# A hybrid decoder layer on one core: two groups of 128x128 transposes taken off TensorE and done by moving 32-row pieces and turning 32x32 blocks

## The chip, the cores and the metric

The kernel runs on one core of a Trainium2 chip. Such a core has five engines that take their own instruction streams in order and meet through semaphores: TensorE (PE in the profile; its weight loads are PEld), VectorE (DVE), ScalarE (ACT), GpSimd (POOL) and SyncE (SP), which here only issues DMAs. The metric is the device time of one execution in microseconds. The median of three runs of the kernel before is 1166.14 us (1165.94 to 1166.46).

## The reference

One decoder layer on x of 2048 tokens by 1024 channels, float32. A normalised x goes through one input projection of 4096 columns. 3072 of them are q, k, v and a gate of 12 attention heads of 64; 1024 feed a short gated convolution. The attention is a mixture of three dilated windows, each over a band of keys; the group outputs are concatenated, projected back to 1024, normalised and added to x.

```python
h = rmsnorm(x, norm_pre_g)
z = jnp.einsum('bsd,de->bse', h, w_in)
q, k, v, g_attn, c_h, c_b, c_c, g_conv = jnp.split(z, cuts, axis=-1)
q = rope(q.reshape(B, S, N_ATTN_HEADS, HEAD_DIM), pos)
k = rope(k.reshape(B, S, N_ATTN_HEADS, HEAD_DIM), pos)
for window, dilation in ((128, 1), (512, 4), (2048, 16)):
    o_i, lse_i = dilated_window_attn(q, k, v, window, dilation)   # scores, exp, sum, p @ v
o = sum over the three of softmax(lse)_i * o_i
attn_out = o * silu(g_attn)
conv_out = c_b * causal_depthwise_conv(c_c * c_h, conv_w) * silu(g_conv)
y = jnp.einsum('bse,ed->bsd', concatenate([attn_out, conv_out]), w_out)
return x + rmsnorm(y, norm_post_g)
```

## The kernel before, in words

The 2048 tokens are cut into four chunks of 512 (`b` = 0 to 3). The 4096 input columns are cut into eight groups of 512 (`grp`): groups 0 and 7 are the convolution, groups 1 to 6 are pairs of heads (k, q, v and gate, 128 columns each). A unit is one group for one chunk: there are 32, of which 24 are attention units, and six of those are of the first chunk. Groups are the outer loop and chunks the inner one, so every fourth attention unit is a first-chunk unit.

Every product is done in two parts, a rounded high part and the rest (`fp32r` tiles with two halves), as three matmuls: high by high, high by low, low by high (L1072 to L1074 for the projection). So whatever is fed to TensorE is first split: ScalarE copies with rounding, VectorE subtracts.

In an attention unit the projections of k, q, v and the gate land in four PSUM banks (`zs`), with channels on the partitions and tokens along the row. k and q are rotated, q on VectorE and GpSimd (L707, L711). v has to stand the other way round, tokens on the partitions: ScalarE (L696; for the first chunk VectorE, L698) brings it to SBUF as `vz`, TensorE turns it by four 128x128 transposes into a PSUM bank (`vt`, L739), and L744 and L745 split it from there. Scores are matmuls with 64 rows (L772 for the dilated windows, L800 for the near one). VectorE takes each row's minimum with the mask (L779, L807), ScalarE the exponential (L783, L811). The probabilities then have queries on the partitions and must be turned before they meet v: `parts` does it for the dilated windows. Its `far` branch, used for chunks 2 and 3 only, turns 32x32 blocks in place on VectorE (L831), which suffices there by the layout; its other branch and `square`, for the near window, use four TensorE transposes into a PSUM bank (L840, L863), from which ScalarE and VectorE split (L845, L846; L870, L873, L877). Then come the products with v (L889; L900 to L902 for the near window), whose results are gathered in SBUF (L920 to L925).

Nothing of the order is left to the hardware. `add` records each step with its engine, an estimated duration, a priority and what it reads and writes; `Plan.schedule` walks through estimated time and gives each engine the ready step of the lowest priority number, and `emit` writes the steps out in that order. A table `SHIFT` nudges the priority of steps by line and unit. So a change of one step's estimate or of the table reorders instructions on all engines. TensorE fills its time between the parts of one unit's attention with the projection of the next unit.

## Time and profile before

| | |
|---|---|
| median of three runs | 1166.14 us |
| the profiled execution: its own time, its span | 1165.18 us, 1163.1 us |
| TensorE, VectorE, ScalarE, GpSimd busy | 1152.5, 960.3, 668.2, 199.7 us |
| transposes of v (L739) | 96 |
| transposes of probabilities outside `far` (L840, L863) | 336 and 192 |
| granted TensorE clock | 0.998 |

The span runs from the first to the last instruction of the program; the device time lies 2.1 us above it. A busy TensorE is counted by overlapping, modelled ends of pipelined matmuls, so its busy share does not tell how tightly the matmuls follow each other; the chain of waits does, where each matmul stands with the time that passes until the next. A VectorE or ScalarE row's mean is the length of one instruction, and back to back they overlap a little, so the group's busy time divided by its count is what one costs in a full queue.

### The profile page before, as it was taken

The page shows a single profiled execution, that of the slowest core. Times are in us where ns is not written, and L with a number is a line of the kernel's source. Part 1 is how long each engine was busy: PE and PEld are TensorE (multiplying, and loading weights), DVE is VectorE, ACT ScalarE, POOL GpSimd, SP SyncE. Part 2 cuts the span into 40 slices and gives each one's busy share as a digit, 9 for nine tenths or more (in the row PEclk, how much of TensorE's full clock was granted, in tenths as well). Part 3 has the DMA queues.
Part 4 walks back from the last instruction along what each step waited for, and adds up shares of the span by engine and source line. Part 5 has one row for each costly group of instructions (what it writes and reads, how often), then busy time and mean ns, then how long its engine had stood idle before and what let it go on. Part 6 is the DMA issues. An engine that isn't in the chain of part 4 may idle for free.

```text
span 1163.1 us, 19964 instructions
## 1 busy us (share of the span) xinstructions
PE 1152.5 (99%) x6422; PEld 958.3 (82%) x6422; DVE 960.3 (83%) x2424; ACT 668.2 (57%) x1722; POOL 199.7 (17%) x158
## 2 busy tenths in 40 slices
PE   9999999999999999999999999999999999999997
PEld 7888888888888888888888888888888888888885
DVE  4744588997999989898999998997999888688876
ACT  6743365665666556666665565674667454544442
POOL 0001112212131222121223221203222103000000
PEclk9999999999999999999999999999999999999999
DMA  9977786787688767777777767688776968445452
GB/s 345 391 278 261 247 247 212 226 236 230 203 247 269 234 215 227 238 223 242 232 245 229 252 167 247 204 272 260 228 243 199 318 208 297 156 149 178 152 165 91
DMA packets 174136, 269.39 MB, mean 232 GB/s; under 512 B 53584, under 2 KB 109904, under 8 KB 174032
## 3 DMA queue, kind: packets, MB, share of 16 engines
q1 hardware_dynamic: 173472, 267.85, 71.1%
q8 instruction: 51, 0.84, 0.3%
q14 instruction: 53, 0.43, 0.1%
q10 hardware_dynamic: 560, 0.27, 0.1%
HBM read 206.77 MB, written 48.69 MB: 220 GB/s over the span
## 4 chain that ended last, share of the span: by engine, by line
PE 94%; DVE 2%; ACT 2%; DMA 1%; SPq 0%; issue 0%; POOL 0%; DVEq 0%; POOLq 0%; ACTq 0%
PE st L1072 20%; PE st L1074 19%; PE st L1073 19%; PE st L889 5%; PE st L1241 4%; PE st L1243 4%; PE st L1242 4%; PE st L772 4%; PE st L800 3%; PE st L840 3%; PE st L901 2%; PE st L863 2%; PE st L548 1%; PE st L902 1%; PE st L739 1%; PE st L900 1%
## 5 line engine op out<-in xcount | busy, mean ns | idle before, releaser
L1072 PE MATMUL st<-xt,w 128*128 128x512 f32 x1020 | 413.3, 405 | 0.0
L1074 PE MATMUL st<-xt,w 128*128 128x512 f32 x1020 | 399.7, 392 | 0.0
L1073 PE MATMUL st<-xt,w 128*128 128x512 f32 x1020 | 398.3, 391 | 0.0
L1074 PEld LDWEIGHTS st<-xt,w 128*128 128x128 f32 x1020 | 191.5, 188 | 42.4
L1072 PEld LDWEIGHTS st<-xt,w 128*128 128x128 f32 x1020 | 191.9, 188 | 40.4 <-issue 6.7
L1073 PEld LDWEIGHTS st<-xt,w 128*128 128x128 f32 x1020 | 192.1, 188 | 31.1
L783 ACT ACTIVATE p<-p,sm 128x128 f32<-128x128 f32 (+3 forms) x192 | 105.9, 553 | 69.2 <-DVE sm L779 69.0
L925 DVE TENSOR_TENSOR uu<-st,uu 64x256 f32<-64x256 f32 x288 | 115.0, 418 | 26.0 <-ACT uu L920 21.8
L920 ACT COPY uu<-st 64x256 f32<-64x256 f32 x192 | 67.2, 367 | 100.7 <-PE st L889 55.9
L1019 POOL TENSOR_TENSOR uu<-uu 128x512 f32<-128x512 f32 x24 | 37.4, 1557 | 359.0 <-DVE uu L1018 359.0
L811 ACT ACTIVATE p<-p,e 128x256 f32<-128x256 f32 (+1 forms) x192 | 94.4, 495 | 5.0 <-DVE e L807 4.8
L779 DVE CUSTOM_DVE_ANT_0 p<-st,cst 128x128 f32<-128x128 f32 (+3 forms) x192 | 82.1, 485 | 16.1 <-PE st L772 15.7
L889 PEld LDWEIGHTS st<-pt,v 128*128 128x128 f32 x480 | 66.7, 191 | 5.6
L807 DVE CUSTOM_DVE_ANT_0 p<-st,cst 128x256 f32<-128x256 f32 (+1 forms) x192 | 66.8, 412 | 4.2 <-PE st L800 4.2
L889 PE MATMUL st<-pt,v 128*128 128x256 f32 x480 | 68.5, 283 | 0.0
L870 ACT ACTIVATE pt<-st 128x512 fp32r<-128x512 f32 (+1 forms) x96 | 51.1, 585 | 24.2 <-PE st L863 20.7
L707 DVE TENSOR_TENSOR rp<-rp,cs 128x512 f32<-128x512 f32 x72 | 53.7, 772 | 12.9 <-DMA rp<-rp 12.7
L707 POOL TENSOR_TENSOR rp<-rp,cs 128x512 f32<-128x512 f32 x24 | 39.5, 1646 | 143.1 <-DMA rp<-rp 96.9
L846 DVE TENSOR_TENSOR pt<-st,pt 128x512 fp32r<-128x512 f32 x84 | 55.9, 683 | 5.0 <-ACT pt L845 4.7
L772 PE MATMUL st<-kk,q 64*128 64x128 f32 (+3 forms) x576 | 56.3, 333 | 0.3 <-DVE v L745 0.2
L772 PEld LDWEIGHTS st<-kk,q 64*128 64x128 f32 x576 | 42.4, 185 | 15.1 <-issue 10.8
L845 ACT CAST pt<-st 128x512 fp32r<-128x512 f32 x84 | 46.8, 581 | 9.0 <-PE st L840 8.4
(262 smaller groups left out, 2045.6 us busy)
## 6 DMA issues: line engine op xcount, KB each, us to landing
xt<-xt SPq DMA_DIRECT2D x256, 512.0 KB
raw<-in_w_in SPq DMA_DIRECT2D x59, 256.0 KB
rp<-rp SPq DMA_DIRECT2D x192, 64.0 KB
vd<-v SPq DMA_DIRECT2D x24, 512.0 KB
v<-vd SPq DMA_DIRECT2D x96, 128.0 KB
ab<-ad SPq DMA_DIRECT2D x48, 256.0 KB
cs<-in_rope SPq DMA_DIRECT2D x19, 512.0 KB
uu<-mix SPq DMA_DIRECT2D x26, 256.0 KB
```

The costliest lines, as they stand in the source:

```text
L707: add(e, dur, pr, lambda o=o, a=a, i=i, eng=eng: eng.tensor_tensor(o.ap, a.ap, cs.ap[:, i], op=ALU.mult), r=[cs], w=[o], port=True)
L772: mm(ps[h].ap[:, (r - r0) * w:(r - r0 + 1) * w], Q.ap[lo:lo + 64, i, r * 128:(r + 1) * 128], KK[j][lo:lo + 64, 4 * r:4 * r + 4, 0:w // 4]. ...
L779: add("DVE", dvet(w) + 0.01, pr + URG, lambda h=h, r=r, P4=P4: vec.tensor_tensor_reduce(P4.ap[:, r, 0:w], ps[h].ap[:, (r - r0) * w:(r - r0 ...
L783: add("ACT", actt(w) + 0.19, pr, lambda h=h, r=r, P4=P4: act.activation(P4.ap[:, r, 0:w], P4.ap[:, r, 0:w], AF.Exp, bias=s4(0, h)[:, r:r + ...
L807: add("DVE", dvet(256) + 0.01, pr + URG, lambda h=h, j=j, g=g, P1=P1: vec.tensor_tensor_reduce(P1.ap[:, g, lo[g]:], ps[h].ap[:, j * 256 + ...
L811: add("ACT", actt(256 - lo[g]) + 0.19, pr, lambda h=h, g=g, P1=P1: act.activation(P1.ap[:, g, lo[g]:], P1.ap[:, g, lo[g]:], AF.Exp, bias=E ...
L889: mm(dst, v, pt.ap[:, i], start=c == 0, stop=c == b, skip_group_check=False)
L920: add("ACT", actt(256, True) + 0.09, pr + URG, lambda: act.copy(cols(a, lo), o()[hi:hi + 64, 0]), r=[O], w=[(a, (h, half))])
L925: fn = lambda l=l: vec.tensor_tensor(cols(a, lo), o()[lo:lo + 64, l], cols(a, lo), op=ALU.add)
L1072: mm(z.ap, w.ap[:, 0, js], xt.ap[:, 0], start=kt == 0, stop=False)
L1073: mm(z.ap, w.ap[:, 0, js], xt.ap[:, 1], start=False, stop=False)
L1074: mm(z.ap, w.ap[:, 1, js], xt.ap[:, 0], start=False, stop=kt == KT - 1)
```

## The change

Two transposes are replaced.

**v.** `vt` and its PSUM bank go. Sixteen ScalarE instructions per unit each take 32 partitions of v (for chunks 1 to 3 straight from the projection's PSUM bank, with the factor 0.5 that L696 applied; for the first chunk from `vz`) and write 128 values a row to another block of 32 partitions of `vq`, so that the 32x32 blocks stand at their transposed places. One VectorE transpose then turns all blocks in place. The split reads `vq` in SBUF.

**The first chunk's probabilities.** For `b` = 0 the TensorE transposes in `parts` and `square` go. A new function `swap` has GpSimd move the blocks in sixteen copies of 32 rows by 128 values, inside the tile of probabilities (the other half of each row is free there), and VectorE turns the blocks. Four such swaps per first-chunk unit, two heads by two kinds of window. The splits read SBUF. Chunks 1 to 3 keep their transposes.

**Beside these.** The very first weight tile is loaded in two halves by two queues and rounded in halves by ScalarE and VectorE; the load of the norm's factors gets a later priority; the table `SHIFT` of 58 entries is replaced by another of 64 (its first line is shown; the rest only reorders).

```diff
+MOVE = 0.22
+SWAP = "POOL"
+ONE, FOUR = (0,), (0,)
 SHIFT = {
-    (-2, 7): 10, (-1, 21): 150, (-1, 45): -60, (0, 40): 150, (1, 13): 1, (1, 16): -90, (2, 5): 80, (2, 13): 90,
+    (-1, 21): 60, (1, 13): -20, (1, 31): -20, (2, 31): -2, (5, 76): 90, (5, 84): -240, (6, 91): 3, (6, 99): 93,
...
             if grp or i:
                 add("DMA", dmat(256), pr, lambda: nc.sync.dma_start(raw.ap, w_in[i, :, grp, :]), w=[raw], land=6.0 if grp else 3.6)
             else:
-                add("DMA", dmat(256), -1.995e6, lambda: nc.sync.dma_start(raw.ap, w_in[i, :, grp, :]), w=[raw], land=3.6)
+                for h, (en, queue) in enumerate((("DMA", nc.sync), ("ACT", nc.scalar))):
+                    cl = slice(256 * h, 256 * h + 256)
+                    add(en, 0.45, -1.995e6, lambda cl=cl, queue=queue: queue.dma_start(raw.ap[:, cl], w_in[0, :, 0, cl]), w=[(raw, h)], land=3.2,
+                        data=0.0 if h else 0.4)
+                    eng, fn = (("ACT", act.copy), ("DVE", vec.tensor_copy))[h]
+                    XW.append(add(eng, actt(256) if h == 0 else dvet(256), URG - 151.9, lambda cl=cl, fn=fn: fn(w.ap[:, 0, cl], raw.ap[:, cl]), r=[(raw, h)], w=[(w, h)]))
+                w_last[:] = [add("DVE", dvet(C) + 0.01, pc, lambda: vec.tensor_tensor(w.ap[:, 1], raw.ap, f(w.ap[:, 0]), op=ALU.subtract),
+                                 r=[raw, (w, 0), (w, 1)], w=[(w, 2)], after=XH, port=True)]
+                return
...
-        vz = Tok(rp_r)
-        if b:
-            add("ACT", actt(C, True), pe + 2, lambda: act.activation(vz.ap, zs[2].ap, AF.Copy, scale=0.5), r=[zs[2]], w=[vz])
-        else:
+        vz, vq = None if b else Tok(rp_r), Tok(rp_r)
+        if not b:
             add("DVE", dvet(C), pe + 2, lambda: vec.scalar_tensor_tensor(
                 vz.ap, zs[2].ap, 0.5, cs.ap[:, 2], op0=ALU.mult, op1=ALU.mult), r=[zs[2], cs], w=[vz])
+        def tile4(t):
+            return t.rearrange("p (r c a) -> p r c a", r=4, c=4)
+        for c in range(4):
+            for a in range(4):
+                z, o = vz if vz else zs[2], slice(32 * c, 32 * c + 32)
+                add("ACT", MOVE if b else MOVE + 0.043, pe + 4 if b else pr, lambda a=a, c=c, z=z, o=o: act.activation(
+                    tile4(vq.ap)[32 * a:32 * a + 32, :, c, :], tile4(z.ap)[o, :, a, :], AF.Copy, scale=0.5 if b else 1.0), r=[z], w=[(vq, (a, c))])
+        add("DVE", dvet(C) + 0.05, pr, lambda: vec.transpose(vq.ap, vq.ap), w=[vq])
...
-        def vt():
-            for r in range(4):
-                nc.tensor.transpose(ps.ap[:, r * 128:(r + 1) * 128], vz.ap[:, r * 128:(r + 1) * 128], ident)
-        add("PE", 0.44, pr, vt, r=[vz, "cst"], w=[ps, (v2, "hold")], mode=2)
...
+        def swap(pp, src, dst):
+            def quarters(o):
+                return pp.ap[:, :, o:o + 128].rearrange("p g (c a) -> p g c a", c=4)
+            for c in range(4):
+                for a in range(4):
+                    add(SWAP, MOVE + 0.043, pr, lambda a=a, c=c: (act.copy if SWAP == "ACT" else pool.tensor_copy)(
+                        quarters(dst)[32 * c:32 * c + 32, :, a], quarters(src)[32 * a:32 * a + 32, :, c]), r=[(pp, g) for g in range(4)], w=[(pp, ("q", a, c))])
+            add("DVE", dvet(C) + 0.05, pr, lambda: vec.transpose(pp.ap[:, :, dst:dst + 128], pp.ap[:, :, dst:dst + 128]),
+                w=[(pp, ("q", a, c)) for a in range(4) for c in range(4)] + [(pp, "t")])
...
+            elif b in FOUR:
+                swap(pp, 0, 128)
...
+                add("ACT", actt(C), pr + URG, lambda: act.copy(pt.ap[:, :, 0, :], flipped()), r=[(pp, "t")], w=[(pt, 0)])
+                add("DVE", dvet(C), pr + URG, lambda: vec.tensor_tensor(
+                    pt.ap[:, :, 1, :], flipped(), f(pt.ap[:, :, 0, :]), op=ALU.subtract), r=[(pp, "t"), (pt, 0)], w=[(pt, 1)], port=True)
...
+            if b in ONE:
+                swap(pp, 128, 0)
+                ps = (pp, "t")
...
+            else:
                 ps = Tok(st_r)
                 def tr():
                     for g in range(4):
                         nc.tensor.transpose(ps.ap[:, g * 128:(g + 1) * 128], pp.ap[:, g, 128:], ident)
...
-    add("ACT", 0.45, -2.1e6, lambda: nc.scalar.dma_start(gp, g_pre), w=["gp"], land=4.0)
+    add("ACT", 0.45, -1.996e6, lambda: nc.scalar.dma_start(gp, g_pre), w=["gp"], land=3.6)
```

Three places show how it moves instructions. First GpSimd at the first attention unit (of the first chunk): `rp` are the rotated q and k, `q` the q tiles, `uu` the gathered results. Before:

```order
L707 TENSOR_TENSOR rp_141<-rp_141,cs_187 128x512
L711 TENSOR_TENSOR rp_141<-rp_141,rp_142 128x512
L727 COPY q_166<-q_165 128x512 x2
L707 TENSOR_TENSOR rp_139<-rp_139,cs_187 128x512
L711 TENSOR_TENSOR rp_139<-rp_139,rp_141 128x512
```

Now, with `p_178` to `p_184` the probabilities of two heads for the dilated and the near windows:

```order
L725 TENSOR_TENSOR rp_141<-rp_141,cs_187 128x512
L729 TENSOR_TENSOR rp_141<-rp_141,rp_142 128x512
L745 COPY q_166<-q_165 128x512 x2
L837 COPY p_178<-p_178 32x4x32 x16
L837 COPY p_179<-p_179 32x4x32 x16
L837 COPY p_183<-p_183 32x4x32 x16
L837 COPY p_184<-p_184 32x4x32 x16
L725 TENSOR_TENSOR rp_141<-rp_141,cs_187 128x512
L729 TENSOR_TENSOR rp_141<-rp_141,rp_139 128x512
```

The 64 pieces stand in one run, and the next unit's q rotation is queued behind them.

Second, VectorE at the same unit, from the first split of probabilities on. Before, the splits read PSUM tiles (`st`):

```order
L846 TENSOR_TENSOR pt<-st_117,pt 128x4x128
L853 TENSOR_TENSOR p_183<-p_183 128x3x128
L853 TENSOR_TENSOR p_184<-p_184 128x3x128
L925 TENSOR_TENSOR uu<-st_112,uu 64x256
L925 TENSOR_TENSOR uu<-st_111,uu 64x256
```

Now (the second to the third swap's transpose):

```order
L839 STREAM_TRANSPOSE p_179<-p_179 128x4x128
L725 TENSOR_TENSOR rp_142<-rp_142,cs_187 128x512
L967 TENSOR_TENSOR uu<-st_118,uu 64x256
L967 TENSOR_TENSOR uu<-st_115,uu 64x256
L865 TENSOR_TENSOR pt<-p_179,pt 128x4x128
L725 TENSOR_TENSOR rp_140<-rp_140,cs_187 128x512
L725 TENSOR_TENSOR rp_139<-rp_139,cs_187 128x512
L839 STREAM_TRANSPOSE p_183<-p_183 128x4x128
```

The transposes stand in VectorE's queue between other work, and the splits now read two SBUF tiles.

Third, TensorE at the same unit, where the second head's products with v (L889, now L931) are reached. Before, eight transposes stand ahead of the projection's next step:

```order
L889 MATMUL st_112<-pt,v_167 128x2x128 x2
L889 MATMUL st_111<-pt,v_167 128x2x128 x2
L1072 MATMUL st_115<-xt_120,w_131 128x512
L1073 MATMUL st_115<-xt_120,w_131 128x512
L1074 MATMUL st_115<-xt_120,w_131 128x512
L840 MATMUL st_113<-cst,p_179 128x128 x4
L863 MATMUL st_118<-cst,p_183 128x128 x4
```

Now only projection follows:

```order
L931 MATMUL st_118<-pt,v_167 128x2x128 x2
L931 MATMUL st_115<-pt,v_167 128x2x128 x2
L1114 MATMUL st_113<-xt_127,w_134 128x512
L1115 MATMUL st_113<-xt_127,w_134 128x512
L1116 MATMUL st_113<-xt_127,w_134 128x512
L1114 MATMUL st_114<-xt_119,w_134 128x512
```

Between the four groups of products of this unit there now stand 18, 15 and 21 projection matmuls; before, 18, 3 and 21 with transposes among them. Over the whole program TensorE loses 192 instructions, and its visits to the 64-row scores, each a stretch of L772 or L800 between other work, rise from 49 to 57.

More of the change, by code (lines that the diff above doesn't have):

```diff
@@ L445, in hybrid_layer @@
     URG = -1.0e5
-    W, w_last = {}, []
+    W, w_last, XW = {}, [], []
     def weights_in(grp, i):
@@ L731, in attn_unit @@
         products = ((0, 0), (0, 1), (1, 0))
-        ps, v2, v1 = Tok(st_r), Tok(v2_r), Tok(v1_r)
+        v2, v1 = Tok(v2_r), Tok(v1_r)
         V2[u], V1[u] = v2, v1
-        def vt():
-            for r in range(4):
-                nc.tensor.transpose(ps.ap[:, r * 128:(r + 1) * 128], vz.ap[:, r * 128:(r + 1) * 128], ident)
-        add("PE", 0.44, pr, vt, r=[vz, "cst"], w=[ps, (v2, "hold")], mode=2)
         def src():
-            return ps.ap.rearrange("p (r h d) -> p r h d", r=4, h=2)
-        add("ACT", actt(C, True), pr + URG, lambda: act.copy(v2.ap[:, :, 0:4:3, :], src()), r=[ps], w=[(v2, 0)])
-        add("DVE", dvet(C), pr + URG, lambda: vec.tensor_tensor(
-            v2.ap[:, :, 1:3, :], src(), f(v2.ap[:, :, 0:4:3, :]), op=ALU.subtract), r=[ps, (v2, 0)], w=[(v2, 1)])
+            return vq.ap.rearrange("p (r h d) -> p r h d", r=4, h=2)
+        add("ACT", actt(C), pr, lambda: act.copy(v2.ap[:, :, 0:4:3, :], src()), r=[vq], w=[(v2, 0)])
+        add("DVE", dvet(C), pr, lambda: vec.tensor_tensor(
+            v2.ap[:, :, 1:3, :], src(), f(v2.ap[:, :, 0:4:3, :]), op=ALU.subtract), r=[vq, (v2, 0)], w=[(v2, 1)], port=True)
         d, dk = v_d[u % 2], ("vd", u % 2)
@@ L851, in square @@
         def square(h):
-            pp, ps, first = P[h, 1], Tok(st_r), int(b == 0)
+            pp, first = P[h, 1], int(b == 0)
             add("DVE", dvet(C), pr, lambda: vec.tensor_tensor(
@@ L859, in blocks, with p4, tr @@
                 return pts[:, sorted((pt_r.index(t.slot) for t in two), reverse=True)[s]]
-            def tr():
-                for g in range(4):
-                    nc.tensor.transpose(ps.ap[:, g * 128:(g + 1) * 128], pp.ap[:, g, 128:], ident)
-            add("PE", 0.436, pr, tr, r=[(pp, g) for g in range(4)] + ["cst"], w=[ps] + [(pt, "hold") for pt in two], mode=2)
-            def p4(lo):
-                return ps.ap[:, lo * 128:].rearrange("p (i c) -> p i c", c=128)
+            if b in ONE:
+                swap(pp, 128, 0)
+                ps = (pp, "t")
+                def p4(lo):
+                    return pp.ap[:, lo:, 0:128]
+            else:
+                ps = Tok(st_r)
+                def tr():
+                    for g in range(4):
+                        nc.tensor.transpose(ps.ap[:, g * 128:(g + 1) * 128], pp.ap[:, g, 128:], ident)
+                add("PE", 0.436, pr, tr, r=[(pp, g) for g in range(4)] + ["cst"], w=[ps] + [(pt, "hold") for pt in two], mode=2)
+                def p4(lo):
+                    return ps.ap[:, lo * 128:].rearrange("p (i c) -> p i c", c=128)
+            on = b in ONE
             for s, pt in enumerate(two):
                 lo = first if not s else 0
-                add("ACT", actt((4 - lo) * 128, True), pr + URG, lambda lo=lo, s=s: act.activation(
-                    blocks(s)[:, lo:, 0, :], p4(lo), AF.Relu, scale=1.0 if s else -1.0), r=[ps], w=[(pt, 0)])
+                add("ACT", actt((4 - lo) * 128, not on), pr + URG, lambda lo=lo, s=s: act.activation(
+                    blocks(s)[:, lo:, 0, :], p4(lo), AF.Relu, scale=1.0 if s else -1.0), r=[ps], w=[(pt, 0)] + [(pt, "hold") for pt in two if on])
                 if s:
```

8 lines of the change are left out of this document (5 added, 3 removed), and 15 rows, old and new, of the table SHIFT.

## The prediction

> **What bounds the kernel now.** I read the page's first lines, then the chain of waits that ended last, then busy time by stage.
>
> ```profile
> span 1163.1 us, 19964 instructions
> PE 1152.5 (99%) x6422; PEld 958.3 (82%) x6422; DVE 960.3 (83%) x2424; ACT 668.2 (57%) x1722; POOL 199.7 (17%) x158
> PE 94%; DVE 2%; ACT 2%; DMA 1%; SPq 0%; issue 0%; POOL 0%; DVEq 0%; POOLq 0%; ACTq 0%
> ```
>
> TensorE is busy for all but 10.6 us and carries 94% of the chain. Whether its instructions really follow each other without gaps is seen in the chain itself, from 283 to 307 us (start, us, what):
>
> ```profile
> 283.87 0.44 PE st L840 x4
> 284.31 0.24 PE st L1072
> ...
> 286.38 0.44 PE st L863 x4
> ...
> 296.16 0.44 PE st L739 x4
> ...
> 302.57 0.43 PE st L1072
> 303.00 0.24 PE st L1073
> ```
>
> A projection matmul takes 0.23 to 0.24 us of TensorE's time and four transposes 0.44 us, one behind the other. So time taken out of TensorE's stream is time off the span, as long as nothing else then ends last. Who could, the stages tell (window; busy us of PE, PEld, DVE, ACT, POOL):
>
> ```profile
> 130.00:330.00 200.00, 199.90 (x1207) 167.14 (x1206) 170.01 (x468) 121.46 (x348) 41.98 (x36) 1.00 0.76 238
> 330.00:530.00 200.00, 200.00 (x1197) 166.92 (x1196) 182.60 (x470) 125.83 (x347) 42.37 (x35) 1.00 0.77 235
> 530.00:730.00 200.00, 200.00 (x1216) 167.79 (x1216) 179.42 (x488) 125.32 (x358) 46.62 (x38) 1.00 0.73 229
> 730.00:930.00 200.00, 199.46 (x1190) 165.56 (x1189) 176.59 (x461) 120.97 (x334) 46.31 (x35) 1.00 0.77 244
> ```
>
> In the 800 us of attention TensorE is full, VectorE is busy for 708.6 us (88.6%), ScalarE for 493.6 and GpSimd for 177.3. VectorE is the only one near.
>
> **The change part by part.**
>
> *TensorE loses* 24 groups of four transposes for v and, in six first-chunk units, two heads by two kinds of window, another 24 groups: 48 x 0.44 = 21.1 us.
>
> *TensorE gains* eight more visits to the scores (49 to 57 in its order). A visit costs what the first matmul behind it shows: 0.43 instead of 0.23 us. 8 x 0.2 = 1.6 us; entering costs something that no quoted row shows, so 0 to 3 us, and I take 2.
>
> *ScalarE* gets 384 moving pieces. No row has 32 rows by 128 values; the nearest are these:
>
> ```profile
> L920 ACT COPY uu<-st 64x256 f32<-64x256 f32 x192 | 67.2, 367 | 100.7 <-PE st L889 55.9 <-PE st L902 40.2 <-DVE q L1147 0.8
> L845 ACT CAST pt<-st 128x512 fp32r<-128x512 f32 x84 | 46.8, 581 | 9.0 <-PE st L840 8.4
> L832 ACT CAST pt<-p 128x512 fp32r<-128x512 f32 x36 | 22.1, 614 | 2.6 <-PE st L889 2.3 <-DVE p L831 0.2
> L696 ACT ACTIVATE rp<-st 128x512 f32<-128x512 f32 x18 | 10.8, 598 | 4.1 <-PE st L1074 3.0 <-POOL rp L711 0.6 <-DMA mix<-uu 0.4
> ```
>
> Of busy time, 512 values a row cost 46.8/84 = 0.56 us and 256 cost 67.2/192 = 0.35, so 128 come to 0.25 on that line, and 0.05 more from SBUF (22.1/36 = 0.61 against 0.56). Bounds: 0.14 (a quarter of 0.56) and 0.35. The 288 pieces from PSUM and 96 from SBUF make 72 + 29 = 101 us, less 10.8 for L696: about 90 us more, 55 to 125 at the bounds, on an engine with 306 us to spare in the attention. Hidden there. What is not free is place: a unit's pieces hold v's PSUM bank for some 4 us instead of 0.6, and the sums, exponentials and gathers queue behind them. The order spreads them and the transposes' own PSUM banks are gone; I take nothing, and leave 0 to 4 us for the range.
>
> *VectorE* gets 48 transposes of 128x512, and its splits read SBUF instead of PSUM.
>
> ```profile
> L831 DVE STREAM_TRANSPOSE p<-p 128x512 f32<-128x512 f32 x36 | 24.3, 696 | 0.6 <-ACT p L783 0.5
> L846 DVE TENSOR_TENSOR pt<-st,pt 128x512 fp32r<-128x512 f32 x84 | 55.9, 683 | 5.0 <-ACT pt L845 4.7
> L833 DVE TENSOR_TENSOR pt<-p,pt 128x512 fp32r<-128x512 f32 x36 | 26.4, 735 | 0.2
> ```
>
> 48 x 24.3/36 = 32.4 us. The 60 splits (24 of v, 36 of probabilities) move from 55.9/84 = 0.67 to 26.4/36 = 0.73: 4 us. VectorE's demand becomes 708.6 + 36 = 745 us of a stretch that TensorE alone would need 781 for: 95%. It still fits on average. In pieces of 25 us:
>
> ```profile
> 425.00:450.00 25.00, 25.00 (x162) 21.00 (x161) 19.94 (x65) 17.46 (x53) 3.59 (x4) 1.00 0.86 271
> 525.00:550.00 25.00, 25.00 (x170) 21.36 (x169) 20.81 (x70) 15.83 (x49) 2.54 (x3) 1.00 0.76 255
> 625.00:650.00 25.00, 25.00 (x152) 20.43 (x151) 24.57 (x67) 18.84 (x52) 3.92 (x5) 1.00 0.85 291
> ```
>
> Stretches of 98% stand beside some of 80%, so the additions find room only where the order moved work. I charge 3 us (0 to 8) of TensorE waiting for a late split.
>
> *GpSimd* gets 384 copies of 32 rows by 128 values, 64 per first-chunk unit. Its nearest rows are a copy of 128x512, and the shortest instruction there is:
>
> ```profile
> L727 POOL CAST q<-q x48: 611/617/1532, 133.0 to 898.4; 128x512 fp32r<-128x512 f32 x48
> 0.24 0.10 POOL L1346 MEMSET const-float32-0.0<- 128x1 f32 x1 [0.24 <-issue]
> ```
>
> Between 0.10 for one value and 0.617 for 512, 128 values lie at 0.10 + 0.52/4 = 0.23 us; bounds 0.10 and 0.62. I take 0.23: 3.7 us a swap, 88 us in all, where GpSimd is three quarters idle. The price is not the engine's time but whom it shuts out. The medians above hide a 1532, and VectorE's two-input product has the counterpart:
>
> ```profile
> L707 DVE TENSOR_TENSOR rp<-rp,cs x72: 649/683/1780, 125.1 to 890.8; 128x512 f32<-128x512 f32 x72
> 132.97 0.62 POOL L727 CAST q<-q 128x512 fp32r<-128x512 f32 x1 [1.79 <-ACT q L722]
> 133.04 1.10 DVE L723 TENSOR_TENSOR q<-rp,q 128x512 fp32r<-128x512 f32 x1
> 295.32 0.67 DVE L711 TENSOR_TENSOR rp<-rp,rp 128x512 f32<-128x512 f32 x1
> 295.54 2.09 POOL L727 CAST q<-q 128x512 fp32r<-128x512 f32 x2 [1.20 <-ACT q L722]
> 295.92 0.68 DVE L723 TENSOR_TENSOR q<-rp,q 128x512 fp32r<-128x512 f32 x1
> ```
>
> At 133 us a VectorE subtraction of two SBUF tiles took 1.10 us because a copy on GpSimd had begun before it; at 295.5 two GpSimd copies took 2.09 us instead of 1.23 because VectorE was in the middle of such work. They exclude each other, whole instructions at a time. In the order of the first attention unit, 3, 4 and 3 two-SBUF-input VectorE instructions stand between the four swap transposes, 0.6 us each by the rows above. So the second, third and fourth swap take 3.7 + 1.8, 3.7 + 2.4 and 3.7 + 1.8 = 5.5, 6.1 and 5.5 us. TensorE has 18, 15 and 21 projection matmuls and four or five products there: about 4.6, 3.9 and 5.6 us. It falls short by 0.9, 2.2 and 0: 3 us. The second first-chunk unit has 21, 21 and 21 matmuls against 5, 5 and 4 such instructions (two of them tiny), short by 1.4, 1.4 and 0. In each of the other four at least one of the distances is 27 matmuls or more, and I charge nothing. Sum 6 us, less what little lead the order leaves: 5 us. Queued behind the run of pieces is the next unit's q rotation (L725, L729), which its scores wait for; behind the last swap TensorE still has products and 18 projection matmuls, 5 us, against two GpSimd instructions, so I add nothing. If a piece costs the lower bound, the swaps wait for nothing; the upper end is the rival below.
>
> *The start.* The first projection waited for the first weight tile and x:
>
> ```profile
> 5.32 0.62 ACT L469 CAST w<-raw 128x512 fp32r<-128x512 f32 x1 [2.15 <-DMA raw<-in_w_in]
> 6.37 1.20 PE L1061 MATMUL st<-xt,w 128*128 128x512 f32 x4 [1.15 <-ACT xt L490]
> 10.86 0.87 PE L548 MATMUL st<-cst,p 128*128 128x128 f32 x6 [0.51 <-DMA p<-in_x]
> ```
>
> Half a cast is 0.3 us less, and half a load lands earlier; but at 10.9 us the loads of x decide, which are reordered. 0.5 us gained, between -1 (a loss) and 1.2 (the idle 1.15). The end is untouched.
>
> *The sum*, against the profiled execution's own 1165.2 us: - 21.1 + 2 + 3 + 5 - 0.5 = - 11.6, so 1153.6. The median of the runs stands 1.0 above that execution: **1154.5 us**.
>
> **The rivals.**
>
> *All of it is hidden.* The pieces are short (0.10 to 0.15 us), the order leaves VectorE enough lead, no wait appears: 1166.1 - 21.1 + 2 - 0.5 = 1146.5. For it: TensorE waits for almost nothing today with VectorE at 89%. Against: 95%, and the exclusion, which exists in the trace.
>
> *GpSimd sets the pace of the first chunk: slower.* Place: the four swaps of each first-chunk unit, in a row in GpSimd's queue. If moving 32 rows costs nearly what moving 128 costs, a piece is 0.40 rather than 0.23 us, a swap 6.4 us, and with 1.8 to 2.4 us of VectorE's exclusive instructions 8.2 to 8.8, against 4 to 5.6 us of TensorE's work between the products in the tight units (8 in the wide ones). Three waits of 3.5 us in two units and of 1.5 us in four make 39 us, and the time 1155 - 5 + 39 = 1189; with 0.32 us a piece the loss halves and the time is 1169. So it decides from about 0.3 us. The Trainium skill, page "SBUF — State Buffer", section "SBUF: two separate sides", says the same of the exclusion: the port pair shared by VectorE and GpSimd is a lock held for the whole instruction, and it meets VectorE instructions with two SBUF inputs. The rows at 133 and 295 us agree (1.10 us for 0.68, 2.09 for 1.23). By that rule the splits that leave PSUM for SBUF (L846, 0.67) join the locked kind, which speaks against this change.
>
> *The gain is given back on VectorE: no change.* With 95% and a lock the first-chunk stretches need more than TensorE leaves: 80% of 33 us before is 26.4, five transposes add 3.4, fourteen locked instructions that wait a whole piece 3.2: 33 us, no slack at all. If each such unit then loses 3 us, 18 of the 21 us return, and the time is 1164.5 to 1168.
>
> **How the numbers follow.** The forecast (1150 to 1163) gets 0.53; hidden, 0.17; no change, 0.10; slower, 0.20. The smallest difference a measurement of this kernel tells from none is about 0.2%, 2.3 us, so: faster 0.70, same 0.10, slower 0.20. The likeliest case's own range is 1148 to 1163. The range for eight in ten starts just under the hidden case and reaches into the slower one, to where a piece costs 0.33 us: 1145 to 1172.
>
> **What would show it.** Right: TensorE's transposes of v gone from the rows and those of probabilities down to 480, its busy time near 1130 us, chain still above 90% TensorE; GpSimd's 384 copies at a median of 0.2 to 0.3 us with a tail where VectorE subtracts; VectorE near 95% in the attention; a few waits of 1 to 3 us of TensorE's products in the first two first-chunk units. Wrong: a median piece above 0.3 us on GpSimd, a chain that runs through L837 and L839, gaps of TensorE in all six first-chunk units, or waits for L716 in the units of chunks 1 to 3, which I price at nothing.

## The result, and the profile after

The changed kernel takes **1224.09 us** (median; 1222.65 to 1225.05) against 1166.3 (1165.94 to 1166.62) before: 1.0495 times as long, 95% interval 1.0478 to 1.0511. The forecast was 1154.5 and the range ended at 1172; the change loses 58 us where 12 were to be gained.

The first lines of its page, and the shares of the chain that ended last:

```profile
span 1222.9 us, 20266 instructions
PE 1164.7 (95%) x6230; PEld 949.7 (78%) x6230; DVE 990.7 (81%) x2473; ACT 766.5 (63%) x2088; POOL 332.5 (27%) x542
PE 49%; DVE 20%; ACT 12%; POOL 9%; DMA 5%; issue 3%; SPq 2%; DVEq 0%; POOLq 0%; ACTq 0%
```

TensorE has 192 instructions fewer, as planned, and still it is busy for 12.2 us longer and idle for 58.2 us instead of 10.6. The chain, which was TensorE's for 94%, now runs through the helpers for half its length. By stage (window; busy us of PE, PEld, DVE, ACT, POOL; then granted clock), where before TensorE had 199.5 to 200 in each:

```profile
130.00:330.00 200.00, 185.83 (x1045) 151.49 (x1045) 156.16 (x417) 128.97 (x387) 86.78 (x160) 0.97 0.68 217
330.00:530.00 200.00, 190.17 (x1102) 154.32 (x1099) 177.50 (x464) 145.36 (x437) 64.63 (x100) 1.00 0.73 224
530.00:730.00 200.00, 189.67 (x1093) 153.34 (x1094) 174.67 (x466) 138.21 (x404) 70.26 (x125) 0.98 0.67 211
730.00:930.00 200.00, 186.46 (x1040) 151.89 (x1038) 172.47 (x449) 139.07 (x414) 81.02 (x134) 0.97 0.70 218
...
150.00:175.00 25.00, 19.07 (x76) 15.17 (x75) 15.51 (x30) 12.46 (x36) 21.64 (x51) 0.86 0.61 196
300.00:325.00 25.00, 18.38 (x74) 14.33 (x73) 15.47 (x34) 11.16 (x32) 20.25 (x41) 0.86 0.54 184
```

In 25 us around the first swaps GpSimd is busy for 87% of the time, TensorE for 76%, VectorE for 62%: no saturation of VectorE, but a queue on GpSimd. The groups of pieces, of the transposes behind them and of the products that wait, with what ended the idle time before them:

```profile
L837 POOL COPY p<-p 32x128 f32<-32x128 f32 x384 | 139.7, 364 | 72.8 <-ACT p L796 45.3
L839 DVE STREAM_TRANSPOSE p<-p 128x512 f32<-128x512 f32 x24 | 17.0, 710 | 53.3 <-POOL p L837 53.3
L943 PE MATMUL st<-pt,v 128*128 128x512 f32 x96 | 41.5, 432 | 25.7 <-DVE pt L915 24.3
```

VectorE stands idle 53.3 us for GpSimd's pieces, and TensorE's near-window products 24.3 us for the split behind that. The pieces themselves (ns: least, median, most; then where in the program), and three swaps in a row with VectorE's work beside the second and the third (start, us):

```profile
L837 POOL COPY p<-p x384: 279/288/4164, 144.5 to 896.0; 32x128 f32<-32x128 f32 x192
...
149.79 20.41 POOL L837 COPY p<-p 32x128 f32<-32x128 f32 x48
...
155.99 0.71 DVE L839 STREAM_TRANSPOSE p<-p 128x512 f32<-128x512 f32 x1 [3.48 <-POOL p L837]
156.63 0.65 DVE L725 TENSOR_TENSOR rp<-rp,cs 128x512 f32<-128x512 f32 x1
157.20 1.40 DVE L967 TENSOR_TENSOR uu<-st,uu 64x256 f32<-64x256 f32 x4
158.53 0.67 DVE L865 TENSOR_TENSOR pt<-p,pt 128x512 fp32r<-128x512 f32 x1
159.12 1.28 DVE L725 TENSOR_TENSOR rp<-rp,cs 128x512 f32<-128x512 f32 x2
163.89 0.71 DVE L839 STREAM_TRANSPOSE p<-p 128x512 f32<-128x512 f32 x1 [3.49 <-POOL p L837]
164.52 0.65 DVE L729 TENSOR_TENSOR rp<-rp,rp 128x512 f32<-128x512 f32 x1
165.21 1.45 DVE L967 TENSOR_TENSOR uu<-st,uu 64x256 f32<-64x256 f32 x4
166.69 0.68 DVE L919 SCALAR_TENSOR_TENSOR pt<-p,pt 128x384 fp32r<-128x384 f32 x1
167.30 0.77 DVE L915 SCALAR_TENSOR_TENSOR pt<-p,pt 128x512 fp32r<-128x512 f32 x1
```

48 pieces in 20.41 us are 6.8 us a swap. Undisturbed, pieces start 0.328 us apart, 5.25 us a swap; over all 24 swaps the mean from first to last piece is 6.9 us, the longest 11.1, since 57 of the 384 pieces took over 0.4 us. Of these, 41 took 0.5 to 0.7, where mostly one of VectorE's two-input instructions (0.65 us) was in the way, and three took 2.4 to 4.2, where several of these followed each other. The order had been made with 0.263 us a piece, 4.2 a swap. The way does not end with the pieces: from the last piece of the second of these swaps (163.9 us) to the end of the split that TensorE waits for (168.1), 0.7 us are the transpose, 1.4 the two splits of probabilities (L919, L915) and 2.1 other work that stands between them in VectorE's queue.

What a long wait does to TensorE besides (its rows from 168 us; idle time before in brackets):

```profile
168.12 0.79 PE L943 MATMUL st<-pt,v 128*128 128x512 f32 x1 [4.72 <-DVE pt L915]
...
169.78 0.63 PE L1114 MATMUL st<-xt,w 128*128 128x512 f32 x1
170.21 0.63 PE L1115 MATMUL st<-xt,w 128*128 128x512 f32 x1
...
173.62 0.63 PE L1114 MATMUL st<-xt,w 128*128 128x512 f32 x1
174.05 0.45 PE L1115 MATMUL st<-xt,w 128*128 128x512 f32 x1
174.34 0.39 PE L1116 MATMUL st<-xt,w 128*128 128x512 f32 x1
174.57 0.40 PE L1114 MATMUL st<-xt,w 128*128 128x512 f32 x1
```

After 4.72 us of waiting the projection's matmuls start 0.43 us apart for 6 us, then 0.23 again.

### The profile page after: what moved, and what is told of

Same layout as the page of the kernel before. It is cut to its first block, busy times and chain, and to the rows that moved or that the text cites. A ratio compares the mean times of both kernels' runs of the same rounds, so it can differ in the third digit from the quotient of the medians.

```text
span 1222.9 us, 20266 instructions
## 1 busy us (share of the span) xinstructions
PE 1164.7 (95%) x6230; PEld 949.7 (78%) x6230; DVE 990.7 (81%) x2473; ACT 766.5 (63%) x2088; POOL 332.5 (27%) x542
## 4 chain that ended last, share of the span: by engine, by line
PE 49%; DVE 20%; ACT 12%; POOL 9%; DMA 5%; issue 3%; SPq 2%; DVEq 0%; POOLq 0%; ACTq 0%
PE st L1114 9%; PE st L1116 9%; PE st L1115 9%; POOL p L837 8%; PE st L1285 4%; PE st L1283 4%; PE st L1284 4%; ACT p L796 3%; ACT rp L716 3%; DVE uu L967 2%; PE st L931 2%; PE st L785 2%; DMA p<-in_x 2%; DVE p L792 1%; ACT p L824 1%
## 5 line engine op out<-in xcount | busy, mean ns | idle before, releaser
L1114 PEld LDWEIGHTS st<-xt,w 128*128 128x128 f32 x1020 | 194.3, 191 | 48.7 <-issue 6.7
L1116 PEld LDWEIGHTS st<-xt,w 128*128 128x128 f32 x1020 | 193.6, 190 | 44.4 <-DVE w L481 1.7
L1115 PEld LDWEIGHTS st<-xt,w 128*128 128x128 f32 x1020 | 194.2, 190 | 33.1 <-DVE xt L565 1.0
L837 POOL COPY p<-p 32x128 f32<-32x128 f32 x384 | 139.7, 364 | 72.8 <-ACT p L796 45.3
L824 ACT ACTIVATE p<-p,e 128x256 f32<-128x256 f32 (+1 forms) x192 | 94.3, 494 | 10.6 <-DVE e L820 10.4
L716 ACT ACTIVATE rp<-st 32x128 f32<-32x128 f32 x288 | 77.2, 268 | 22.2 <-issue 9.5
L725 POOL TENSOR_TENSOR rp<-rp,cs 128x512 f32<-128x512 f32 x24 | 32.3, 1347 | 193.7 <-DMA rp<-rp 87.4
L931 PE MATMUL st<-pt,v 128*128 128x256 f32 x480 | 73.5, 293 | 12.0 <-DVE pt L865 5.6
L931 PEld LDWEIGHTS st<-pt,v 128*128 128x128 f32 x480 | 67.4, 195 | 21.8 <-DVE pt L865 6.4
L745 POOL CAST q<-q 128x512 fp32r<-128x512 f32 x48 | 39.7, 830 | 99.9 <-ACT q L740 55.8
L943 PE MATMUL st<-pt,v 128*128 128x512 f32 x96 | 41.5, 432 | 25.7 <-DVE pt L915 24.3
L729 POOL TENSOR_TENSOR rp<-rp,rp 128x512 f32<-128x512 f32 x24 | 36.9, 1537 | 91.9 <-DVE rp L725 91.3
L839 DVE STREAM_TRANSPOSE p<-p 128x512 f32<-128x512 f32 x24 | 17.0, 710 | 53.3 <-POOL p L837 53.3
```

The lines of the kernel that those rows point to most:

```text
L716: add("ACT", MOVE if b else MOVE + 0.043, pe + 4 if b else pr, lambda a=a, c=c, z=z, o=o: act.activation(tile4(vq.ap)[32 * a:32 * a + 32, ...
L824: add("ACT", actt(256 - lo[g]) + 0.19, pr, lambda h=h, g=g, P1=P1: act.activation(P1.ap[:, g, lo[g]:], P1.ap[:, g, lo[g]:], AF.Exp, bias=E ...
L837: add(SWAP, MOVE + 0.043, pr, lambda a=a, c=c: (act.copy if SWAP == "ACT" else pool.tensor_copy)(quarters(dst)[32 * c:32 * c + 32, :, a], ...
L931: mm(dst, v, pt.ap[:, i], start=c == 0, stop=c == b, skip_group_check=False)
L1114: mm(z.ap, w.ap[:, 0, js], xt.ap[:, 0], start=kt == 0, stop=False)
L1115: mm(z.ap, w.ap[:, 0, js], xt.ap[:, 1], start=False, stop=False)
```

## The experiments

### Fewer pieces, same order

Four runs leave pieces out and keep the changed kernel's order of everything else. A lambda that emits a piece gets `a == c and` (4 of 16 are moved) or `a != c and` (12 of 16), so part of the values or probabilities is not turned.

```diff
-    ... lambda a=a, c=c: (act.copy if SWAP == "ACT" else pool.tensor_copy)(
+    ... lambda a=a, c=c: a == c and (act.copy if SWAP == "ACT" else pool.tensor_copy)(
```

On GpSimd alone, 4 of 16:

> Twelve of the sixteen GpSimd pieces of each swap are left out (the first chunk's probabilities are then not all moved); the order of everything else is the changed kernel's. In the changed kernel a piece takes 0.288 us and the next starts 0.328 us after it, so a swap of sixteen lasts 5.2 us or more; four last 1.3 us. Theory G (GpSimd's swaps pace the first chunk): the waits of TensorE in the six first-chunk stretches (about 43 us) and the half-clock stretches behind them (30 us at 0.5) go, 1224 falls to about 1170. Theory S (ScalarE's pieces make the splits late): nearly nothing changes, above 1210. Theory O (the order itself leaves TensorE idle): a few us, above 1210.

On ScalarE alone, 4 of 16:

> Twelve of the sixteen ScalarE pieces of each unit's v are left out (v is then not all moved); the order is the changed kernel's. A piece takes 0.268 us (0.308 from SBUF) and starts 0.279 (0.319) after the one before, so ScalarE gets 3.3 us a unit back. Theory G: only the waits outside the first chunk shrink, 1224 falls to 1200 at most. Theory S: most of the loss is in ScalarE's queue, 1224 falls to 1180 or below. Theory O: above 1210.

On both, 4 of 16:

> Both cuts together: four of sixteen pieces on GpSimd and on ScalarE, the order of everything else the changed kernel's. Theories G and S: no piece is late any more and TensorE is full as it was, 1166 - 21 + 2 = about 1147 to 1152. Theory O: the order keeps TensorE idle even with quick pieces, 1160 or more.

On both, 12 of 16, about what the order had reckoned with:

> Twelve of sixteen pieces on both engines (the four with equal source and destination block are left out). So a swap or a move takes what the order was built on: 12 x 0.328 = 3.9 us against 16 x 0.263 = 4.2, and 12 x 0.279 = 3.3 against 16 x 0.22 = 3.5. If the loss is the overrun of each piece over that estimate, the time is within 10 us of the run with four pieces. If it is the mutual exclusion of GpSimd's pieces and VectorE, which the estimate does not count, most of the loss stays: 1195 or more.

Measured, with the ratio to the kernel before, run beside it: GpSimd 1181.45 us (1.0123, 1.0094 to 1.0153), ScalarE 1211.08 (1.0377, 1.0347 to 1.0407), both 1168.18 (1.001, 0.9998 to 1.0021), 12 of 16 on both 1186.16 (1.0164, 1.0134 to 1.0193). So three quarters of GpSimd's pieces cost 42.6 us and three quarters of ScalarE's 13.0; the sum, 55.6, is what both together give, 55.9. TensorE's wait for the near-window split (L943 for L915), 24.3 us in the changed kernel, falls to 2.9 us where GpSimd's pieces are left out and stays at 22.8 where ScalarE's are:

```profile
L943 PE MATMUL st<-pt,v 128*128 128x512 f32 x96 | 40.8, 425 | 23.8 <-DVE pt L915 22.8
```

So theory G has the place right, and not the price: the time was expected at about 1170, and the expectation's 43 us of waits in the six first-chunk stretches are 31 in the trace. The run with ScalarE's pieces out and the one with both came out as theory O had them (above 1210; 1160 or more); theory S forecast neither, and G not the second. The run with 12 of 16 lies between its two outcomes (within 10 us of 1168; 1195 or more): a quarter fewer pieces brings 38 of the 58 us back, so the loss starts steeply where a swap overruns its place, but 18 remain. Its swaps still took 5.5 us on average and up to 9.8, against 4.2 in the order's costs, because pieces still met VectorE's instructions. The groups in the run with both at 4 of 16:

```profile
span 1167.5 us, 19695 instructions
PE 1143.2 (98%) x6230; PEld 939.1 (80%) x6230; DVE 989.3 (85%) x2473; ACT 688.3 (59%) x1800; POOL 235.6 (20%) x254
...
L839 DVE STREAM_TRANSPOSE p<-p 128x512 f32<-128x512 f32 x24 | 16.7, 701 | 0.9 <-POOL p L837 0.9
L943 PE MATMUL st<-pt,v 128*128 128x512 f32 x96 | 38.6, 402 | 2.2 <-DVE pt L915 1.6 <-DVE sm L792 0.3 <-issue 0.3
L931 PE MATMUL st<-pt,v 128*128 128x256 f32 x480 | 70.9, 287 | 5.4 <-DVE pt L878 3.4 <-DVE pt L857 1.9
```

VectorE's wait falls from 53.3 to 0.9 us. The same 6230 instructions of TensorE are busy for 21.5 us less than in the changed kernel, idle for 33.9 less; the granted clock explains most of the first: before its last matmul TensorE stood at half clock for 34 us there, 17 us lost at most, and for 3.4 us here, 1.7 lost. And a second reading, which the prediction had not seen: even with the pieces all but gone, the kernel is no faster than before. TensorE has 9.3 us less busy time and 13.7 us more idle time than before the change (24.3 against 10.6), in many small waits.

### Is what remains VectorE's new work?

```diff
-        ... vec.transpose(vq.ap, vq.ap), w=[vq])
+        ... vec.transpose(vq.ap[:, 0:32], vq.ap[:, 0:32]), w=[vq])
-            ... vec.transpose(pp.ap[:, :, dst:dst + 128], pp.ap[:, :, dst:dst + 128]),
+            ... vec.transpose(pp.ap[:, 0, dst:dst + 32], pp.ap[:, 0, dst:dst + 32]),
```

> The kernel of the run with 4 of 16 pieces on both engines (1168.2 us, span 1167.5, TensorE 1143.2 us busy, so some 24 us idle), and in it the 72 block transposes of VectorE cut from 512 columns to 32 (of each, 15 of 16 columns are left unturned). That takes some 72 x 0.6 = 43 us from VectorE, which is 92 to 98% busy in the stretches where TensorE still idles. Theory V (what is left after the pieces is VectorE's added work: it is full, and its splits come late): TensorE's idle time falls by 14 us or more, to 1147-1154. Theory O (the order in which the work is written leaves TensorE waiting, for buffers and work of its own order, whatever the helpers take): TensorE still idles 16 us or more, 1160-1168.

1164.43 us (0.9986, 0.9975 to 0.9996). The expectation had miscounted: there are 48 such transposes, not 72, and they got 24 us shorter in place of 43; VectorE's busy time as a whole fell by only 17 us (989.3 to 972.2), because others of its instructions got longer:

```profile
L718 DVE STREAM_TRANSPOSE rp<-rp 128x32 f32<-128x32 f32 x24 | 4.8, 200 | 0.6 <-ACT rp L716 0.6
L839 DVE STREAM_TRANSPOSE p<-p 128x32 f32<-128x32 f32 x24 | 4.7, 201 | 0.1
```

Scaled to 17 us, V would have taken 5 us or more off TensorE's idle time; the time fell by 3.7, and TensorE still idles 22.5 us in the profiled execution (the slowest of eight) against 24.3. That is O's forecast (1160 to 1168, 16 us of idle time or more): the transposes' load on VectorE is a part at most. What the rest of these small waits comes from, no run settles.

### What a piece's price hangs on

```diff
-                    tile4(vq.ap)[32 * a:32 * a + 32, :, c, :], tile4(z.ap)[o, :, a, :], ...
+                    tile4(vq.ap)[o, :, a, :], tile4(z.ap)[o, :, a, :], ...
-                        quarters(dst)[32 * c:32 * c + 32, :, a], quarters(src)[32 * a:32 * a + 32, :, c]), ...
+                        quarters(dst)[32 * a:32 * a + 32, :, c], quarters(src)[32 * a:32 * a + 32, :, c]), ...
```

> The changed kernel with all its pieces, of the same size and number and in the same order, but each copied to the rows that it was read from, so that rows are not swapped and four pieces in a row stay on one block of 32 rows (the values are then not transposed as a whole). Theory B (a change of the block of rows is what costs: other ScalarE instructions start 95 ns before the one ahead ends, these pieces 11 ns after): ScalarE's pieces start 0.18-0.20 us apart inside a block, GpSimd's under 0.30, and the time falls by 13 us or more, to 1211 or less. Theory P (the price is that of an instruction of 32 rows, wherever it writes): still 0.28 and 0.33 us apart, 1219-1228.

1214.86 us (1.0415, 1.0394 to 1.0435). ScalarE's rows of the same stretch, first of the changed kernel and then of this run:

```profile
165.21 0.27 ACT L716 ACTIVATE rp<-st 32x128 f32<-32x128 f32 x1
165.38 0.61 ACT L912 ACTIVATE pt<-p 128x512 fp32r<-128x512 f32 x1
166.02 3.90 ACT L716 ACTIVATE rp<-st 32x128 f32<-32x128 f32 x14
```

```profile
165.97 0.27 ACT L716 ACTIVATE rp<-st 32x128 f32<-32x128 f32 x1
166.14 0.61 ACT L912 ACTIVATE pt<-p 128x512 fp32r<-128x512 f32 x1
166.66 2.71 ACT L716 ACTIVATE rp<-st 32x128 f32<-32x128 f32 x14
```

Fourteen pieces take 2.71 instead of 3.90 us. Within a block of rows they start 0.159 us apart (median of the run 0.161) where the changed kernel has 0.279. At the edges between two blocks, where the rows change from one piece to the next though no piece moves its data to other rows, they start 0.269 us apart: what counts is the change between pieces, not the move within one. So B for ScalarE, and 9.2 us of the time; B's 13 us or more were too much, and 1214.9 lies between the two forecasts. GpSimd's stay at 0.329 us apart: P for GpSimd.

Whether the rows read or the rows written decide, the exchanged loops tell; here all is moved as the change wants it.

```diff
-        for c in range(4):
-            for a in range(4):
+        for a in range(4):
+            for c in range(4):
                 z, o = vz if vz else zs[2], slice(32 * c, 32 * c + 32)
```

> The changed kernel with the two loops over ScalarE's pieces of the values exchanged: the same 16 pieces a unit, moved as the change wants them, but four in a row now write one block of 32 rows and read four different ones (in the changed kernel four in a row read one block and write four). Theory W (the block written decides whether the next piece may start before the one ahead ends): pieces 0.16 us apart inside a block as in the run without a move between rows (0.159), 0.28 at its edges, and about the time of that run, 1211-1217. Theory R (the block read, or any difference of the two, decides): 0.28 us apart throughout, 1220-1228.

1224.47 us (1.0493, 1.0458 to 1.0528), and again 14 pieces in 3.90 us:

```profile
166.60 3.90 ACT L716 ACTIVATE rp<-st 32x128 f32<-32x128 f32 x14
```

R: whichever side changes its block, the next piece doesn't start before the one ahead has ended. Each of the sixteen pieces has its own pair of blocks, so one after another they always change one of the two, and no order of theirs takes this price away.

### Orders that know the prices

The order is made from costs written in the kernel. In the next runs these costs are changed and the table that shifts priorities is made anew, by search.

The swaps alone on GpSimd; the values go through TensorE as before the change:

```diff
-                    add(SWAP, MOVE + 0.043, pr, lambda a=a, c=c: ...
+                    add(SWAP, 0.328 if SWAP == "POOL" else 0.319, pr, lambda a=a, c=c: ...
-                add("ACT", MOVE if b else MOVE + 0.043, pe + 4 if b else pr, lambda a=a, c=c, z=z, o=o: act.activation(
...
-        add("DVE", dvet(C) + 0.05, pr, lambda: vec.transpose(vq.ap, vq.ap), w=[vq])
...
+        add("PE", 0.44, pr, vt, r=[vz, "cst"], w=[ps, (v2, "hold")], mode=2)
```

> Half of the change: the first chunk's probabilities go by GpSimd's pieces and VectorE's transpose (24 swaps, about 24 x 0.44 = 10.6 us less TensorE work than before), the values are turned by TensorE as before the change. GpSimd's piece stands in the order's costs at its measured 0.328 us, and the table of numbers that sets the order is made anew for it. Theory O (the order, made with a piece at 0.263 us, is what lost): an order that knows the price puts the pieces early enough, 1154-1163. Theory G (GpSimd's 5.25 us a swap paces the first chunk whatever the order): 1180 or more. Theory V (VectorE's added work eats the gain): 24 transposes of 0.7 us are a third of it, 1163-1168.

The whole change with measured prices:

```diff
-                add("ACT", MOVE if b else MOVE + 0.043, pe + 4 if b else pr, lambda ...
+                add("ACT", 0.279 if b else 0.319, pe + 4 if b else pr, lambda ...
-                    add(SWAP, MOVE + 0.043, pr, lambda a=a, c=c: ...
+                    add(SWAP, 0.328 if SWAP == "POOL" else 0.319, pr, lambda a=a, c=c: ...
```

> The whole change, with the pieces in the order's costs at their measured prices (0.328 us on GpSimd, 0.279 and 0.319 us on ScalarE in place of 0.263, 0.22 and 0.263) and the table of numbers made anew; the work and the instructions are those of the changed kernel. Theory O: 1155-1164, the loss of 58 us being one of order and price. Theory G: 1185 or more, since GpSimd's pieces take as long as before. Theory V: 1166-1175, no better than the run in which the pieces were cut to a quarter (1168).

1187.9 us (1.0183, 1.0168 to 1.0198) for the swaps alone and 1197.4 (1.0262, 1.0245 to 1.0279) for the whole: with a new price and a new table the whole change gets back 27 of its 58 us, and both times are as G forecast (1180, 1185 or more). That does not show that GpSimd sets the rest: price and table changed together, and the control below shows what a new table alone can cost. 0.328 us is what a piece takes alone. In these two runs a swap took 7.3 and 6.9 us on average, 0.45 and 0.43 us a piece, since the pieces still meet VectorE:

```profile
L1013 POOL COPY p<-p 32x128 f32<-32x128 f32 x384 | 140.5, 366 | 59.6 <-ACT p L972 39.4 <-DVE p L1061 4.0
...
DVE p L1015 <- POOL p L1013: 23.2, 12, 3.5
```

(From the swaps alone; L1013 are the swaps' pieces, L1015 VectorE's transpose; in this wait: total us, times, longest.) VectorE waits for them 23.2 us in place of 53.3, and 22.4 us in the run of the whole.

So three runs with 0.43 us for GpSimd's pieces: the swaps dealt to two engines, a control, and the values alone.

```diff
-                    add(SWAP, MOVE + 0.043, pr, lambda a=a, c=c: (act.copy if SWAP == "ACT" else pool.tensor_copy)(
+                    en = ("POOL", "ACT")[(a + c) % 2]
+                    add(en, (0.43, 0.319)[en == "ACT"], pr, lambda a=a, c=c, en=en: (act.copy if en == "ACT" else pool.tensor_copy)(
-    return max(0.11, n / 2400 + 0.0134)
+    return max(0.11, n / 2400 + 0.0134) * 1.01
-    return n / 960.0 + 0.067
+    return (n / 960.0 + 0.067) * 1.01
```

> The half of the change that swaps the first chunk's probabilities, with the 16 pieces of a swap dealt in turn to GpSimd and ScalarE (8 and 8; a whole swap took GpSimd 6.9 us on average, 5.25 at best, since about three pieces a swap sit 0.65 us behind VectorE); the values are turned by TensorE as before the change. The order's costs hold 0.43 us for a GpSimd piece (6.9 / 16) and 0.319 for a ScalarE piece, 1% more for TensorE and VectorE than before, and the table of numbers is made anew. TensorE has 24 groups less, 10.6 us. Theory O (price and order): swaps of about 3.5 us come in time, 1149-1160, below the kernel before. Theory G (any swap through GpSimd in the first chunk keeps TensorE waiting): 1175 or more, like the run with the swaps alone on GpSimd (1188).

The control is the kernel before with the last two costs and a table made anew:

> Control: the kernel before with none of the change, the same 1% on the order's costs for TensorE and VectorE and its table of numbers made anew in the same way and as long. TensorE waits only some 3 us in the kernel before, so a better order has little to take away there: what it saves are TensorE's changes between scores and other work. Theory O: 1155-1166; the part of the gain of the run with split swaps that is not its swaps is this run's gain. If this run is as fast as the run with split swaps, the swaps are worth nothing.

The values alone (`ONE, FOUR = (), ()`, the pieces at 0.279 and 0.319, and the same two costs):

> The other half of the change: the values go by ScalarE's pieces and VectorE's transpose (24 units, 10.6 us less TensorE work), the probabilities are turned by TensorE as before. The order's costs hold the pieces at their measured 0.279 and 0.319 us, 1% more for TensorE and VectorE, and the table is made anew. Theory O: 1153-1162. Theory S (4.5 to 5.1 us of ScalarE's pieces ahead of each values' transpose make the splits late whatever the order): 1168 or more.

Split swaps 1170.14 us (1.003, 1.002 to 1.004), control 1174.79 (1.0085, 1.0061 to 1.011), values alone 1175.44 (1.0081, 1.0066 to 1.0096). The control is the surprise: a new table costs the kernel before itself 8.7 us, so a part's worth can't be read against the kernel before. Against the control the values earn nothing and the split swaps 4.7 us. The split swaps lie between what O (1160 at most) and G (1175 or more) expected; from the swaps on GpSimd alone (1187.9) they differ in engines, costs and table at once, and what each of these is worth is not told apart. The values alone came out as S said (1168 or more), but the control, without any piece, is as slow, so that is no evidence for S.

A table made against durations that are a little too short may leave no slack. The last pair has dearer helpers in the costs, by what the control's trace had them take beyond their costs:

```diff
+        if land is None and dur > 0.3:
+            dur += 0.02 if eng == "ACT" else 0.04 if eng == "DVE" and port else 0.25 if eng == "POOL" and port else 0.0
         op.eng, op.dur, op.prio, op.fn, op.toks = eng, dur, prio, fn, []
...
-                add("DVE", dvet(256), pr + URG, fn, r=[O], w=[(a, (h, half))])
+                add("DVE", dvet(256) + 0.055, pr + URG, fn, r=[O], w=[(a, (h, half))])
```

> The half of the change that swaps the first chunk's probabilities, in pieces dealt to GpSimd and ScalarE as in the run at 1170.1 us, with a table made against dearer helpers: on top of that run's costs each instruction of ScalarE above 0.3 us costs 0.02 more, of VectorE with two SBUF inputs 0.04, of GpSimd 0.25, the sums of the products 0.055 (all from what these instructions took beyond their costs in the trace of the control run), so that the order leaves the helpers slack. Theory O (the swaps are a gain once order and prices are sound): below the kernel before by 3 us or more, 1150-1163, and below the control of this call by as much. Theory H (what TensorE saves comes back as waits for helpers, since each swap makes the helpers' way longer): 1164-1172, and within 3 us of the control.

> Control: the kernel before, none of the change, with the same dearer helpers in the order's costs and its table made anew in the same way. Theory O: slower than the run with split swaps by 3 us or more. Theory H: within 3 us of it. In both it should lie nearer to the kernel before than the first control did (1174.8), if it was a table without slack that cost that one 8.7 us.

Split swaps 1170.55 us (1.0034, 1.0021 to 1.0048), control 1167.91 (1.0016, 1.0007 to 1.0025). The control has come back to within 1.3 us of the kernel before; the split swaps are 2.6 us behind it, where with the first tables they were 4.7 ahead. First lines of the split swaps, then of the control:

```profile
span 1166.5 us, 20170 instructions
PE 1149.3 (99%) x6326; PEld 948.3 (81%) x6326; DVE 979.7 (84%) x2449; ACT 729.5 (63%) x1914; POOL 273.1 (23%) x350
...
PE st L737 <- DMA p<-in_x: 3.4, 2, 3.1
PE st L1108 <- DVE pt L1055: 3.1, 2, 1.6
```

```profile
span 1165.6 us, 19938 instructions
PE 1155.2 (99%) x6422; PEld 959.0 (82%) x6422; DVE 960.8 (82%) x2424; ACT 670.6 (58%) x1722; POOL 191.8 (16%) x158
...
PE st L730 <- DMA p<-in_x: 1.6, 2, 1.3
```

In these two executions, whose spans are only 0.9 us apart (the one of the split swaps is the fastest of its five), TensorE is busy 5.9 us less and idle 6.8 us more (17.2 against 10.4). 1.8 us of that is the start, waiting for x, which is not the swaps' doing; 3.1 us are waits for a split of probabilities that the control has not. The result fits H, and the control fits the want of slack as the reason for the 8.7 us; but each is one table, made once. The two pairs together put the worth of well-ordered swaps between -3 and +5 us, less than a table can win or lose. No complete kernel here beats the one before.

What stays open: why the changed kernel with quick pieces is no faster than before; a search that finds no good order doesn't show that there is none; the values alone were not run with slack in the table, nor the split swaps with the start of the kernel before.

## Why the prediction was wrong

*How the miss of 69.6 us adds up.* The step that failed is the 5 us charged to TensorE waiting for the swaps: three quarters of GpSimd's pieces alone cost 42.6. ScalarE's pieces, taken at nothing, cost 13.0. The other 18.7 us remain with quick pieces, a quarter of them still in (1168.2 against 1149.5, the forecast without those 5): there the gain itself did not come, and the cause is open. The next paragraphs take the steps in turn.

*What bounds the kernel: right, and its warning was missed.* With TensorE full and the rest behind it, each late result is time. The prediction used that for the gain (21 us out of the stream), and not for the length of the way that the probabilities now take through three other engines.

*TensorE's gain: the work left, the gain did not come.* 192 instructions are gone (its transposes of probabilities are down to 432; the prediction's 480 was a slip). With quick pieces TensorE's busy time is 9.3 us lower, not 19, and it idles 13.7 us more than before the change. What the eight visits cost was not measured apart.

*GpSimd's piece: the first error in the charge for the swaps.* It was worked out as 0.23 us, on a line between a one-value fill (0.10) and a copy of 128x512 (0.617). Measured: 0.288 long, 0.328 from start to start. The line's lower end was another kind of instruction, and the 0.04 us to the next one weren't counted. 16 x 0.1 us make 1.6 us a swap. By the prediction's own rival a piece at this price makes about 1170, so more than its price was wrong.

*The exclusion: right in kind, too small in place.* Foreseen for the second to fourth swap of the first two units, 1.8 to 2.4 us each; measured 1.7 us on average for every swap. The same lock that the Trainium skill describes ("SBUF — State Buffer", "SBUF: two separate sides") is what the rows show: pieces of 0.65 us and more beside 0.65 us products. But a piece that met several of these in a row waited for all of them (4.16 us at 734.9 us into the program, beside seven). "In each of the other four I charge nothing" was wrong: TensorE's waits make 4.1 to 6.6 us in each of the six first-chunk stretches (31 us together, and 17 elsewhere in the 800 us of attention).

*The price of a wait: missing.* The prediction counted a wait at its length. Here a wait of 4.7 us was followed by 6 us of matmuls at half speed. The Trainium skill, "TensorE: Matmul & The Clock Gate", "Part 1: The HAM clock gate", has half rate after an idle window of about 3.4 us. The trace agrees in kind; it shows half speed after eight waits, and five of them were shorter, 1.9 to 2.4 us (880, 900, 607, 818 and 669 us into the program). By granted clock it makes at most 15 of the 56 us between the changed kernel and the one with quick pieces.

*ScalarE's pieces "hidden, I take nothing": wrong, 13 us for three quarters of them.* The duration was well guessed (0.25 and 0.30 us, measured 0.268 and 0.308), and the engine had room (63% busy). Unforeseen was that pieces don't overlap, 0.279 us apart, 4.5 us a unit; the sentence that they hold a unit's PSUM bank "for some 4 us" had the mechanism, but gave it no price. (The lower bound for ScalarE's work was a slip of no consequence: 384 x 0.14 less 10.8 is 43 us, not 55.)

*VectorE at 95%: not reached.* 681 of 800 us in the changed kernel, 730 (91%) with quick pieces; taking 17 us off it brought 3.7.

*The start*: no gain is shown. The changed kernel has 47.34 us of TensorE's work in the first 50 in place of 47.17, the one with quick pieces, which starts in the same way, 45.94.

*The rivals.* "GpSimd sets the pace of the first chunk", with 0.20, is what happened, its bound of 0.3 us included; its own price at 0.32 us, 1169, was 55 us too low, for the lock in every swap, half speed after the wait, ScalarE's 13 us and the gain that did not come. The prediction's signs of being wrong are in the rows: the chain runs through L837 and L839, TensorE waits in all six first-chunk units, and VectorE waits for L716 (13.6 us, six of the nine times in units of chunks 1 to 3). The one on a median piece above 0.3 us misses by its measure: a piece is 0.288 us long, and the distance between starts is what counts. "No change", with 0.10, is the time of the kernel with quick pieces, though VectorE's transposes explain little of it.

## What to carry to other kernels

Where one engine is full and the work taken from it goes through three others in a row, price the way, not the engines' totals: so many small instructions, from start to start and with the lock they meet, against the time until the full engine wants the result. A small instruction's price should come from a row with the same engine, kind and rows, and where none exists, the upper bound deserves the larger chance. An order made from costs must be made from costs that hold on the chip, and any remade order needs a control with none of the change: here a new table moved the unchanged kernel by 8.7 us.
